# Raising the scheduling priority of PSUM evacuations, and a third buffer for gate and rotation, in a two-layer hybrid attention block

## The chip, the cores and the metric

The kernel runs on one core of one Trainium2 chip. The metric is the device time of one execution in microseconds (us), the median over several runs. The instructions are issued on five in-order engines: PE (matrix products and transposes, results in PSUM), ACT (pointwise functions and copies), DVE (vector arithmetic and reductions), POOL (elementwise arithmetic on SBUF) and SP (which only issues DMAs here).

## The reference, cut to what matters

Two layers act on 512 latent tokens and 256 context tokens of width 1024. Each layer normalises, projects once to 3584 columns, runs three groups of attention heads on parts of the projection, multiplies each group's output with a gate, and projects back:

```
h  = rms_norm(x, norm_g[l]) * (1 + sc) + sh          # same for the context: hc
qa, ka, va, ga, qb, kb, vb, gb, qn, kn, vn, gn = split_proj(h @ w_in[l])
ya = rms_norm(diff_attend(rope(qa), rope(ka), va)) * silu(ga)     # group A, 4 heads, two maps each
yb = gqa_attend(rope(qb), rope(kb), vb) * silu(gb)                # group B, 6 heads, 2 key heads
yn = neighbourhood_attend(qn, kn, vn, bias) * silu(gn)            # group C, 6 heads
x  = x + gt * (concat(ya, yb, yn) @ w_out[l])
```

q and k are normalised per head (rms_norm) first; queries of the latents also read the keys of the context. In the first layer the context gets its own attention and update; in the second only its keys and values are needed.

## The kernel before, in words

**Projection.** Tokens are cut into six tiles of 128 (j = 0 to 3 latent, 4 and 5 context), and the columns into ten chunks of 256 or 384 (`CH`, L37): a0 and a1 hold q, k, v of group A, b0 and b1 of B, c0, c1 and c2 of C, and ga, gb and gn the three gates. `proj` (L709) takes one chunk and one token tile at a time. It takes a PSUM tile with the tag "p" (`psP`, two buffers, L122), issues 24 products into it (`mm3`, L676: high and low parts of activations and weights, three products for each of eight slices of 128 input features), and calls `evac` (L657), which empties the tile. Weights arrive as pieces in a ring (`WStream`, L60): a DMA, a rounding copy on ACT (L89) and a subtraction on POOL or DVE (L92).

**Evacuation.** What reads the PSUM tile depends on the chunk:
- `qk_evac` (L451), for q and k: one ACT copy to the SBUF tile "xn" (L462). Then the square (L464) into "sq", its sum (L465), and the rotation in `qk_turn` (L477): two POOL products into a tile "tb" (L485, L487), one product (L489) and one sum that reads "tb" (L490). Every two tiles an inverse root (L163) is formed on POOL, and `qk_finish` (L494) scales, splits to 16 bits and issues a transposing DMA (L534).
- `v_evac` (L573), for v: an ACT scaling to 16 bits (L585) and a DVE operation that forms the rest (L586).
- `gate_evac` (L597), for the gates: tanh on ACT into a tile "sq" (L600), then a DVE operation that reads "sq" and the PSUM tile and writes a tile "tb" (L602); for ga one more product on POOL (L605); then a DMA stores "tb" to DRAM (L606). It is read back when the heads' output is gated (`gate_load`, L961).

The tag "tb" has two buffers. The rotation, the gates, the modulation blocks at the start (`ada_pair`, L196) and some residual loads (L1122) share them. The tags "xn" and "sq" have five and two.

**Heads.** `attn` (L972) goes through units of one head and 128 queries (the context's units hold several heads; a head of group A has two maps): scores on PE (`stage_S`, L780), their maximum on DVE (L827, or L824 with bias) and its scaling on ACT (L829), the exponential on ACT (L841), a rounding to 16 bits on ACT (L861) and the rest on POOL (L862), a transposing DMA (L864), the product with v on PE (`stage_PV`, L867), and the output arithmetic in `pv_evac` (L903). For group A a DVE operation (L857) first combines the two maps.

**Order.** `both` (L1064) writes the heads of one group and the projection of the next chunks alternately: during A the chunks b0, b1, gb; during B c0, c1, c2, gn; during C the output projection. That is only the order in which instructions are written down. Each one gets a number that grows along this order, and the order of each engine is fixed before the run by a simulated timeline: an engine that is free takes, of the instructions whose inputs and buffers are ready in that simulation, the one with the lowest number. A `prio(off)` around a call (L132) adds `off` to the numbers of the instructions issued inside. Before the change this is used for `stage_S` (-400), for `y_build` and `y_pair` (-600), for the next layer's `build_h` (-800) and for one prefetch (-100). The evacuations have their plain numbers. On the chip every engine works through its list in that order, and waits where an input is late.

Of the kernel before, what the change touches and what calls it, by code (L numbers as in the profile page):

```python
# [10 lines left out]
F32 = mybir.dt.float32  # L11
# [4 lines left out]
AF = mybir.ActivationFunctionType  # L16
ALU = mybir.AluOpType
# [99 lines left out]
def tile_hybrid_block(ctx: ExitStack, tc: tile.TileContext, xT_d, cT_d, ng_d, w_ada, bT_d, w_in, w_out,  # L117
# [7 lines left out]
    V, A, G, PE, SP = nc.vector, nc.scalar, nc.gpsimd, nc.tensor, nc.sync  # L125
# [3 lines left out]
    def sb(shape, dt=F32, tag="", bufs=1):  # L129
        return pool.tile(shape, dt, tag=tag, bufs=bufs, name=tag)  # L130

    def prio(off):  # L132
        def deco(f):
            def g(*a, **k):
                tc.cur_priority += off
                try:
                    return f(*a, **k)
                finally:
                    tc.cur_priority -= off
            return g  # L140
        return deco

    ident = sb([128, 128], F32, "ident")
    ones = sb([128, 128], F32, "ones")
    colD = sb([128, 1], F32, "colD")
# [33 lines left out]
    def new_mods(l):  # L179
        mods[l] = (sb([128, KT, 2], F32, "mA", 2), sb([128, KT, 2], F32, "mB", 2), sb([128, KT, 2], F32, "mG", 2))  # L180
# [15 lines left out]
    def ada_pair(load):  # L196
        l, bs, ts = load
        if l not in mods:
            new_mods(l)
        ps = psV.tile([128, 512], F32, tag="pv", name="ada")  # L200
        for i in range(2):
            for r in range(2):
                for g in range(4):
                    PE.matmul(ps[32 * g:32 * g + 32, 128 * i:128 * i + 128], lhsT=cS[:, 4 * r + g, :],
                              rhs=ts[2 * i + r][:, g, :], start=(r == 0), stop=(r == 1), tile_position=(0, 32 * g))
        t = sb([128, 256], F32, "tb", 2)
        V.tensor_copy(t, ps[:, 0:256])
        for i in range(2):
            PE.matmul(ps[:, 256 + 2 * i:258 + 2 * i], lhsT=t[:, 128 * i:128 * i + 128], rhs=sel, start=True, stop=True)
        for i, b in enumerate(bs):  # L210
            w, kt = divmod(b, 8)
            src = ps[:, 256 + 2 * i:258 + 2 * i]
            if w == 1:
                V.tensor_scalar(out=mods[l][0][:, kt, :], in0=src, scalar1=bT1[:, l, kt:kt + 1],
                                scalar2=ng[:, l, kt:kt + 1], op0=ALU.add, op1=ALU.mult)
            else:
                V.tensor_scalar(out=mods[l][1 if w == 0 else 2][:, kt, :], in0=src, scalar1=bT[:, l, b:b + 1],
                                scalar2=None, op0=ALU.add)
# [64 lines left out]
    for l in range(DEPTH):  # L283
        for c in ORDER:
            n, c0 = CH[c][1], sum(v[1] for k, v in CH.items() if k < c)
            pidx[l, c] = []
            for q in range(4):
                src = w_in[l, q, :, 2 * c0:2 * c0 + 2 * n].rearrange("p (k n) -> p k n", n=n)
                pidx[l, c].append(len(pieces))
                pieces.append(("w", n, 2, [(src, 0, n)]) + ((v_norm(l, c, q),) if c in VCOL else ()))  # L290
        for part in ("ab", "n"):
            for oc in range(4):
                pidx[l, part, oc] = []
                for k0, nk in OKT[part]:
                    src = w_out[l, oc, :, k0:k0 + nk, :]
# [150 lines left out]
    def bc(ap, shape):  # L446
        return ap.to_broadcast(shape)
# [3 lines left out]
    def qk_evac(l, g, w, j, ps, last, tag=None):  # L451

        d = 32 if g == "A" else 64
        nh = 2 if (g, w) == ("B", "k") else NH[g]
        n = nh * d
        b = batch.setdefault((g, w), [])
        if not b:
            b.append(sb([128, 24], F32, "ss", 4))
        ss = b[0]
        i = len(b) - 1  # L460
        xt = sb([128, 384], F32, "xn", 5) if tag is None else sb([128, 768], F32, *tag)[:, 0:384]
        A.copy(out=xt[:, :n], in_=ps)  # L462
        sq = sb([128, 384], F32, "sq", 2)
        A.activation(out=sq[:, :n], in_=xt[:, :n], func=AF.Square, scale=QS)  # L464
        V.tensor_reduce(out=ss[:, nh * i:nh * i + nh], in_=sq[:, :n].rearrange("p (h d) -> p h d", d=d),  # L465
                        axis=AX.X, op=ALU.add)
        b.append((j, xt))
        qk_turn(l, g, w, j, xt, nh, d)
        if not last:
            return  # L470
        del batch[g, w]
        m = (len(b) - 1) * nh
        r = rsqrt(ss[:, :m], m, 1.0, d * EPS * QS * QS)
        for i, (j, xt) in enumerate(b[1:]):
            qk_finish(l, g, w, j, xt, r[:, nh * i:nh * i + nh], nh, d)

    def qk_turn(l, g, w, j, xt, nh, d):  # L477

        c, n = lc[l], nh * d
        xn = xt[:, :n].rearrange("p (h d) -> p h d", d=d)  # L480
        if g in "AB" and j < 4:
            t1, t2 = c["T", g, w]
            h = d // 2
            tb = sb([128, 384], F32, "tb", 2)[:, :n].rearrange("p (h d) -> p h d", d=d)
            G.tensor_tensor(out=tb[:, :, 0:h], in0=xn[:, :, h:d], in1=bc(t2[:, j:j + 1, 0:h], [128, nh, h]),  # L485
                            op=ALU.mult)
            G.tensor_tensor(out=tb[:, :, h:d], in0=xn[:, :, 0:h], in1=bc(t2[:, j:j + 1, h:d], [128, nh, h]),  # L487
                            op=ALU.mult)
            share("T").tensor_tensor(out=xn, in0=xn, in1=bc(t1[:, j:j + 1, :], [128, nh, d]), op=ALU.mult)  # L489
            share("R").tensor_tensor(out=xn, in0=xn, in1=tb, op=ALU.add)  # L490
        elif (g, w) != ("C", "q"):
            G.tensor_tensor(out=xn, in0=xn, in1=bc(c["g"][g + w].unsqueeze(1), [128, nh, d]), op=ALU.mult)
# [80 lines left out]
    def v_evac(l, c, g, j, ps, h0, nh):  # L573
        s = st[g]
        if (l, c) not in scaled:
            scaled.add((l, c))
            a = v_scale(l, c)
            for h in range(h0, h0 + nh):
                s["si", h] = a[:, 6:7]
                s["si2"] = a[:, 5:6]  # L580
            s["s", c] = a[:, 7:8]
        sc = s["s", c]
        src = ps.rearrange("p (h d) -> p h d", d=64)
        hi, lo = s["V"][:, j, h0:h0 + nh, 1:65], s["V"][:, j, h0:h0 + nh, 65:129]
        A.activation(out=hi, in_=src, func=AF.Copy, scale=sc)  # L585
        V.scalar_tensor_tensor(out=lo, in0=src, scalar=sc, in1=hi, op0=ALU.mult, op1=ALU.subtract)  # L586

    gates = set()

# [7 lines left out]
    def gate_evac(l, c, j, ps):  # L597
        f0, n = GCOL[c]
        t = sb([128, 384], F32, "sq", 2)[:, :n]
        A.activation(out=t, in_=ps, func=AF.Tanh, scale=0.5)  # L600
        y = sb([128, 384], F32, "tb", 2)[:, :n]
        V.scalar_tensor_tensor(out=y, in0=t, scalar=1.0, in1=ps, op0=ALU.add, op1=ALU.mult)  # L602
        if c == "ga":
            y4 = y.rearrange("p (h d) -> p h d", d=64)
            G.tensor_tensor(out=y4, in0=y4, in1=bc(lc[l]["sub"].unsqueeze(1), [128, 4, 64]), op=ALU.mult)  # L605
        SP.dma_start(out=g_d[l][128 * j:128 * j + 128, f0:f0 + n], in_=y)  # L606
        gates.add((l, c, j))
# [495 lines left out]
    def out_parts(l):  # L1103

        if l + 1 == DEPTH:
            for h in range(2):
                st["part", h] = (big(1, F32, [128, KT // 2, NL]) if h else
                                 st["stB"][:, 0:2048].rearrange("p (k t) -> p k t", t=NL))
                for q in range(2):
                    SP.dma_start(out=st["part", h][:, 2 * q:2 * q + 2, :], in_=x1_d[:, 4 * h + 2 * q:4 * h + 2 * q + 2, :])  # L1110
        for oc in range(4):
            if oc == 1 and l + 1 < DEPTH:
                layer_consts(l + 1)
                h_bound(l + 1)
            for st_ in range(2 if l == 0 else 1):
                _, t0, w = streams[st_]
                for b in range(2):
                    db = 2 * oc + b
                    if l + 1 == DEPTH:
                        xo = st["part", db // 4][:, db % 4, :]  # L1120
                    else:
                        xo = sb([128, 576], F32, "stg", 2) if st_ == 0 else sb([128, 384], F32, "tb", 2)  # L1122
                        xo = xo[:, 0:w]
                        SP.dma_start(out=xo, in_=xT_d[:, db, t0:t0 + w])
                    ps = psP.tile([128, 512], F32, tag="p", name="op")
                    out_mm(ps, l, "ab", oc, b, st_, b == 1 and (st_ == 1 or l))
                    V.scalar_tensor_tensor(out=xo, in0=ps[:, 0:w], scalar=mods[l][2][:, db, st_:st_ + 1], in1=xo,
                                           op0=ALU.mult, op1=ALU.add)
                    if l + 1 < DEPTH:
                        SP.dma_start(out=part_d[:, db, t0:t0 + w], in_=xo)  # L1130
                    yield
                    yield
# [238 lines left out]
```

## Time and profile before

| what | value |
|---|---|
| median of 3 runs | 922.99 us (919.12 to 923.62) |
| the profiled execution | 921.41 us |
| its span, from first to last instruction | 919.6 us |
| mean granted TensorE clock | 0.957 of full speed |
| busy ACT, POOL | 593.1 us (64%), 544.1 us (59%) |
| ACT exponential L841, 200 instructions | 166.3 us |
| POOL rest of the probabilities L862, 138 instructions | 205.4 us |

The page gives the busy time of every engine as a share of the span. A view by windows gives the same for any stretch, with the granted clock of PE beside it. The view of waits lists which instruction waited for which, with the total, the number of times and the longest. The timeline shows single instructions with their start and duration; in brackets stands the idle time before one and what ended it. PEld are the weight loads of PE, which run beside its products.

### The profile page before, as it was taken

What the parts mean: (1) busy time and instruction counts of PE and PEld (TensorE: products, weight loads), DVE (VectorE), ACT (ScalarE), POOL (GpSimd) and SP (SyncE); (2) the same over time, 40 slices, a digit from 0 to 9 for tenths busy, and PEclk for the clock granted to TensorE, in tenths of its full rate; (3) what the DMA queues carried; (4) which work ended last, traced back from release to release, by engine and by line L of the source; (5) the groups of instructions that cost most, each with busy time, mean ns of one, the idle gap of its engine ahead of it and who ended that gap; (6) DMA issues with size and microseconds to landing.
All of it is one profiled execution on the core that took longest, in us unless ns stands there. A gap on an engine that the chain in (4) does not pass through costs nothing. (4 is left out here: it accounts for less than half of the span.)

```text
span 919.6 us, 17947 instructions
## 1 busy us (share of the span) xinstructions
PE 824.1 (90%) x6386; PEld 705.7 (77%) x6386; DVE 681.9 (74%) x1306; ACT 593.1 (64%) x1269; POOL 544.1 (59%) x503
## 2 busy tenths in 40 slices
PE   6898988896998899896999989989959999987988
PEld 3687877795987688784778879978848878875667
DVE  4985787988778866557755798789977976876743
ACT  5334577785887687577663445478758888878630
POOL 1638855899698565434421036939988886654310
PEclk9999998998999999998999989999979999998999
DMA  9924895645879997998798723784547789999642
GB/s 325 320 88 127 202 198 151 139 102 136 190 156 212 223 213 178 223 262 217 145 232 245 246 76 92 173 206 98 123 131 188 133 199 255 205 233 250 129 87 88
DMA packets 307193, 165.46 MB, mean 180 GB/s; under 512 B 256544, under 2 KB 275232, under 8 KB 306976
## 3 DMA queue, kind: packets, MB, share of 16 engines
q1 hardware_dynamic: 307104, 164.33, 74.5%
q8 instruction: 50, 0.82, 0.4%
q14 instruction: 39, 0.32, 0.1%
HBM read 86.55 MB, written 15.47 MB: 111 GB/s over the span
## 5 line engine op out<-in xcount | busy, mean ns | idle before, releaser
L862 POOL TENSOR_TENSOR hl<-p,hl 128x768 f16<-128x768 f32 (+3 forms) x138 | 205.4, 1492 | 170.7 <-ACT hl L861 159.0
L679 PE MATMUL proj<-whi,bigL 128*128 128x384 f32 (+1 forms) x592 | 203.0, 344 | 8.5 <-DVE tb L602 5.1
L680 PE MATMUL proj<-wlo,bigL 128*128 128x384 f32 (+1 forms) x592 | 199.6, 337 | 0.8 <-POOL wlo L92 0.7
L681 PE MATMUL proj<-whi,bigL 128*128 128x384 f32 (+1 forms) x592 | 196.7, 334 | 0.0
L841 ACT ACTIVATE p<-sc,nb,gsc 128x768 f32<-128x768 f32 (+3 forms) x200 | 166.3, 845 | 10.9 <-DVE p L857 4.6
L827 DVE TENSOR_REDUCE mx<-sc 128x1 f32<-128x768 f32 (+2 forms) x128 | 118.6, 931 | 30.3 <-PE sc L775 30.3
L861 ACT CAST hl<-p 128x768 f16<-128x768 f32 (+3 forms) x144 | 104.4, 725 | 46.4 <-DMA pt<-hl 29.9
L679 PEld LDWEIGHTS proj<-whi,bigL 128*128 128x128 f32 x592 | 115.0, 194 | 18.9 <-DVE tb L602 7.2
L680 PEld LDWEIGHTS proj<-wlo,bigL 128*128 128x128 f32 x592 | 115.6, 195 | 3.9 <-POOL wlo L92 1.5
L681 PEld LDWEIGHTS proj<-whi,bigL 128*128 128x128 f32 x592 | 114.5, 194 | 2.7 <-issue 1.6
L92 POOL TENSOR_TENSOR wlo<-raw,whi 128x768 fp32r<-128x768 f32 (+1 forms) x44 | 82.8, 1889 | 31.7 <-ACT whi L89 28.1
L89 ACT CAST whi<-raw 128x768 fp32r<-128x768 f32 (+1 forms) x104 | 80.1, 779 | 25.3 <-DMA raw<-in_w_in_dram 11.1
L897 PEld LDWEIGHTS <-pt 128*128 128x128 f16 x736 | 66.4, 100 | 36.8 <-DMA pt<-hl 23.2
L679 PE MATMUL proj<-whi,bigC 128*128 128x384 f32 (+2 forms) x224 | 75.6, 337 | 1.0 <-ACT xn L462 1.0
L92 DVE TENSOR_TENSOR wlo<-raw,whi 128x768 fp32r<-128x768 f32 (+1 forms) x60 | 61.5, 1028 | 19.4 <-ACT whi L89 18.1
L680 PE MATMUL proj<-wlo,bigC 128*128 128x384 f32 (+2 forms) x224 | 74.3, 332 | 0.0
L163 POOL TENSOR_TENSOR rsqb<-rsqb,half 128x12 f32<-128x12 f32 (+2 forms) x25 | 68.5, 2739 | 9.7 <-DVE rsqb L162 8.8
L681 PE MATMUL proj<-whi,bigC 128*128 128x384 f32 (+2 forms) x224 | 73.6, 331 | 0.0
L898 PEld LDWEIGHTS <-pt 128*128 128x128 f16 x736 | 66.8, 100 | 4.6 <-issue 2.4
L775 PE MATMUL sc<-bigL 128*128 128x512 f16 (+4 forms) x184 | 46.5, 314 | 18.5 <-ACT p L841 18.1
L897 PE MATMUL pv<-vA,pt 128*128 128x128 f16 (+2 forms) x424 | 52.1, 230 | 12.1 <-DMA pt<-hl 12.1
L829 ACT ACTIVATE nb<-mx,lnp,gsc 128x1 f32<-128x1 f32 (+1 forms) x104 | 39.9, 385 | 33.3 <-DVE mx L827 22.5
(327 smaller groups left out, 2038.6 us busy)
## 6 DMA issues: line engine op xcount, KB each, us to landing
raw<-in_w_in_dram SPq DMA_DIRECT2D x64, 384.0 KB, 3.9
adw<-in_w_ada_dram SPq DMA_DIRECT2D x68, 256.0 KB, 3.5
raw<-in_w_out_dram SPq DMA_DIRECT2D x16, 384.0 KB, 4.5
raw<-in_w_in_dram SPq DMA_DIRECT2D x16, 256.0 KB, 3.0
g_d<-tb SPq DMA_DIRECT2D x20, 192.0 KB, 2.8
gt<-g_d SPq DMA_DIRECT2D x18, 192.0 KB, 3.6
hl<-in_w_ada_dram SPq DMA_DIRECT2D x12, 256.0 KB, 4.8
pt<-in_w_ada_dram SPq DMA_DIRECT2D x12, 256.0 KB, 4.9
```

Of the source, the lines that this page charges most:

```text
L89: self.nc.scalar.copy(out=hi, in_=raw2)
L92: self.share("W").tensor_tensor(out=lo, in0=raw2, in1=hi.bitcast(F32), op=ALU.subtract)
L163: G.tensor_tensor(out=y, in0=x, in1=half[:, 0:n], op=ALU.pow)
L679: PE.matmul(ps, lhsT=xh, rhs=hi, start=(kt == 0), stop=False)
L680: PE.matmul(ps, lhsT=xh, rhs=lo, start=False, stop=False)
L681: PE.matmul(ps, lhsT=xl, rhs=hi, start=False, stop=(kt == KT - 1))
L827: V.tensor_reduce(out=mx[:, 0:ns], in_=ps[:, 0:w * ns].rearrange("p (a b) -> p a b", b=w), axis=AX.X, op=ALU.max)
L841: A.activation(out=p[:, w * x:w * x + w], in_=u["ps", i][:, w * x:w * x + w], func=AF.Exp, bias=u["nb", i][:, x:x + 1], scale=lc[l]["sc"][ ...
L861: A.copy(out=hl[:, 0:n], in_=p)
L862: lo_eng.tensor_tensor(out=hl[:, n:2 * n], in0=p, in1=hl[:, 0:n], op=ALU.subtract)
L897: PE.matmul(po[r, :], lhsT=pt[:, b, r], rhs=V_[:, vt, c0:129], start=first, stop=False)
L898: PE.matmul(po[r, 0:65 - c0], lhsT=pt[:, nb + b, r], rhs=V_[:, vt, c0:65], start=False, stop=stop)
```

## The change

Five instructions that read a projected tile in PSUM are issued through `first = prio(-1200)`: the copy of q and k, both operations of v, and tanh and the product of the gate. Their numbers drop by 1200, below those of all the heads' operations near them, `stage_S` with its -400 included. The square, the rotation and all that follows keep their numbers. The tag "tb" gets three buffers in place of two, wherever it is used.

```
+    first = prio(-1200)
@@ ada_pair @@
-        t = sb([128, 256], F32, "tb", 2)
+        t = sb([128, 256], F32, "tb", 3)
@@ qk_evac @@
-        A.copy(out=xt[:, :n], in_=ps)
+        first(A.copy)(out=xt[:, :n], in_=ps)
@@ qk_turn @@
-            tb = sb([128, 384], F32, "tb", 2)[:, :n].rearrange("p (h d) -> p h d", d=d)
+            tb = sb([128, 384], F32, "tb", 3)[:, :n].rearrange("p (h d) -> p h d", d=d)
@@ v_evac @@
-        A.activation(out=hi, in_=src, func=AF.Copy, scale=sc)
-        V.scalar_tensor_tensor(out=lo, in0=src, scalar=sc, in1=hi, op0=ALU.mult, op1=ALU.subtract)
+        first(A.activation)(out=hi, in_=src, func=AF.Copy, scale=sc)
+        first(V.scalar_tensor_tensor)(out=lo, in0=src, scalar=sc, in1=hi, op0=ALU.mult, op1=ALU.subtract)
@@ gate_evac @@
-        A.activation(out=t, in_=ps, func=AF.Tanh, scale=0.5)
-        y = sb([128, 384], F32, "tb", 2)[:, :n]
-        V.scalar_tensor_tensor(out=y, in0=t, scalar=1.0, in1=ps, op0=ALU.add, op1=ALU.mult)
+        first(A.activation)(out=t, in_=ps, func=AF.Tanh, scale=0.5)
+        y = sb([128, 384], F32, "tb", 3)[:, :n]
+        first(V.scalar_tensor_tensor)(out=y, in0=t, scalar=1.0, in1=ps, op0=ALU.add, op1=ALU.mult)
@@ out_parts @@
-                        xo = sb([128, 576], F32, "stg", 2) if st_ == 0 else sb([128, 384], F32, "tb", 2)
+                        xo = sb([128, 576], F32, "stg", 2) if st_ == 0 else sb([128, 384], F32, "tb", 3)
```

## The prediction

> **What bounds the kernel now.** I read the page's head first, then the busy time by windows, then who PE waits for, and last the timeline at the two places that stand out. The head:
>
> ```profile
> span 919.6 us, 17947 instructions
> PE 824.1 (90%) x6386; PEld 705.7 (77%) x6386; DVE 681.9 (74%) x1306; ACT 593.1 (64%) x1269; POOL 544.1 (59%) x503
> ```
>
> PE is busy 90% of the span and no other engine over 74%. Time is lost where PE stands still, 919.6 - 824.1 = 95.5 us in all. The windows say where. Columns: stretch, its length, busy us of PE, PEld, DVE, ACT and POOL with counts, granted PE clock, DMA share, GB/s.
>
> ```profile
> core 0: us, PE busy (x) PEld busy (x) DVE busy (x) ACT busy (x) POOL busy (x), PEclk, DMA share, GB/s
> 140.00:250.00 110.00, 95.47 (x696) 85.73 (x696) 94.46 (x143) 81.53 (x203) 89.76 (x90) 0.95 0.61 136
> 250.00:345.00 95.00, 89.17 (x733) 75.23 (x734) 73.14 (x144) 75.96 (x145) 70.84 (x60) 0.98 0.91 202
> 595.00:700.00 105.00, 87.13 (x656) 76.79 (x655) 91.33 (x137) 77.38 (x183) 83.62 (x86) 0.92 0.64 153
> 700.00:800.00 100.00, 96.85 (x758) 85.31 (x757) 75.19 (x109) 85.81 (x152) 76.69 (x57) 1.00 0.90 196
> 214.00:222.00 8.00, 2.81 (x12) 1.89 (x12) 6.25 (x7) 4.49 (x10) 8.00 (x5) 0.86 0.60 172
> 222.00:228.00 6.00, 5.92 (x22) 5.92 (x23) 4.90 (x6) 3.17 (x7) 5.76 (x5) 0.62 0.80 197
> 670.00:683.00 13.00, 3.10 (x19) 1.42 (x18) 8.55 (x10) 7.58 (x19) 13.00 (x11) 0.64 0.42 106
> 683.00:688.00 5.00, 5.00 (x17) 5.00 (x18) 4.94 (x7) 1.45 (x4) 4.04 (x4) 0.56 0.54 141
> ```
>
> The heads of group A run in the first and the third stretch, and PE stands 14.5 and 17.9 us there; the stretches behind them lose 5.8 and 3.2 us. Most of A's idle time lies in two holes: 214 to 222 (8.00 - 2.81 = 5.2 us) and 670 to 683 (13.00 - 3.10 = 9.9 us). After each hole PE is busy throughout, at a granted clock of 0.62 and 0.56. What PE waits for, over the whole span (total, times, longest):
>
> ```profile
> PE sc L775 <- ACT p L841: 20.2, 18, 3.9
> PE pv L897 <- DMA pt<-hl: 16.7, 21, 3.1
> ...
> PE proj L679 <- DVE tb L602: 5.1, 4, 2.8
> PE yt L640 <- DVE tb L602: 4.4, 1, 4.4
> ...
> PE proj L679 <- ACT xn L462: 2.1, 4, 1.0
> ```
>
> Evacuations are named for under 12 us, the heads' chain for 36.9. But a wait on the heads is a wait only because PE had nothing else in its list at that place. The second hole shows why it had nothing. PE first:
>
> ```profile
> 662.72 0.34 PE L681 MATMUL proj<-whi,bigL 128*128 128x384 f32 x1
> ...
> 663.24 0.34 PE L681 MATMUL proj<-whi,bigL 128*128 128x384 f32 x1
> ...
> 682.97 0.69 PE L679 MATMUL proj<-whi,bigL 128*128 128x384 f32 x1 [2.79 <-DVE tb L602]
> ```
>
> The first gate tile (gb, token tile 0) is complete at 663.24 + 0.34 = 663.6. One slice of three products takes 663.24 - 662.72 = 0.52 us, so a tile of eight slices takes 4.2. The next-but-one tile, which needs the same PSUM buffer, starts at 682.97, when L602 has emptied it. The evacuation of that first tile:
>
> ```profile
> 671.34 0.48 ACT L600 ACTIVATE sq<-proj 128x384 f32<-128x384 f32 x1
> ```
>
> ```profile
> 682.37 0.54 DVE L602 SCALAR_TENSOR_TENSOR tb<-sq,proj 128x384 f32<-128x384 f32 x1
> ```
>
> Tanh starts 671.34 - 663.58 = 7.8 us after the products, behind the heads' ACT work. Then 682.37 - 671.82 = 10.6 us pass before L602, although DVE is idle for 4.4 of the 13 us in this hole. What holds L602 is its output buffer:
>
> ```profile
> 651.85 0.65 POOL L485 TENSOR_TENSOR tb<-xn,t2Bq 128x192 f32<-128x192 f32 x1
> ...
> 657.78 0.91 POOL L485 TENSOR_TENSOR tb<-xn,t2Bq 128x192 f32<-128x192 f32 x1
> ...
> 666.02 0.99 POOL L490 TENSOR_TENSOR xn<-xn,tb 128x384 f32<-128x384 f32 x1
> ...
> 675.88 0.58 POOL L485 TENSOR_TENSOR tb<-xn,t2Bq 128x192 f32<-128x192 f32 x1
> ...
> 679.45 0.99 POOL L490 TENSOR_TENSOR xn<-xn,tb 128x384 f32<-128x384 f32 x1
> ```
>
> A rotation holds "tb" from L485 to its L490. Two are open from 657.78 on, so both buffers are taken; the one freed at 667.0 is kept for the rotation of 675.88, which was written down earlier than the gate, and the other is free at 680.4. L602 follows 2 us later. In the first hole the same two gate tiles are held; there tanh comes at 221.0 and L602 at 221.5 and 224.1:
>
> ```profile
> L600 ACT ACTIVATE sq<-proj x3: 478/480/491, 221.0 to 228.6; 128x384 f32<-128x384 f32 x3
> ```
>
> ```profile
> L602 DVE SCALAR_TENSOR_TENSOR tb<-sq,proj x2: 553/554/555, 221.5 to 224.1; 128x384 f32<-128x384 f32 x2
> ```
>
> **The change, part by part.** It adds no instruction and removes none; it moves five kinds of them forward in the lists of ACT and DVE and gives "tb" a third buffer.
>
> (1) The holes, 5.2 + 9.9 = 15.1 us. With the priority, tanh of the first gate tile follows the product at about 664; with the third buffer L602 follows tanh; the PSUM tile is free near 665 in place of 682.9, and PE, done with the second gate tile before the hole, has the third and fourth to fill it with: 2 x 4.2 = 8.4 us of the 9.9, and one tile covers most of the 5.2. What is late next is the weights of the following chunk, whose L92 is on POOL, and POOL is busy 13.00 of 13.00 us in this hole. Work done early counts in full only if PE is the bound where it comes from: it is busy 96.85 of 100 us from 700 to 800 and 89.17 of 95 from 250 to 345. I take two thirds, 10.1 us; the bounds are 0 and 15.1.
>
> (2) The clock behind the holes. 6 us at 0.62 and 5 us at 0.56 lose 6 x 0.38 + 5 x 0.44 = 4.5 us against a full clock. It goes with (1): 3.0 us, bounds 0 and 4.5. The Trainium skill (TensorE: Matmul & The Clock Gate, "Part 1: The HAM clock gate") says that the clock halves after an idle window of about 3.4 us and returns after a busy one; an estimate from that page is 2 x 1.7 = 3.4 us for two holes, two thirds of which would make the forecast 0.7 us later. The trace agrees in direction, 0.62 and 0.56 behind the holes against 1.00 from 700 to 800.
>
> (3) The two named waits outside the holes: L640, an output transpose that needs the PSUM buffer of the last gate tile (4.4), and the copies L462 (2.1), 6.5 us. An evacuation still has to wait for the instruction in progress and to run, so I take half, 3.3; bounds 0 and 6.5.
>
> (4) The price. Each evacuation now goes ahead of the heads' exponential, maximum and rounding. Durations (min, median, max in ns), and what ACT waited for in these instructions:
>
> ```profile
> L462 ACT COPY xn<-proj x56: 243/460/488, 81.5 to 800.2; 128x384 f32<-128x384 f32 x32, 128x256 f32<-128x256 f32 x12, 128x128 f32<-128x128 f32 x12
> L600 ACT ACTIVATE sq<-proj x30: 362/478/514, 113.1 to 830.4; 128x384 f32<-128x384 f32 x20, 128x256 f32<-128x256 f32 x10
> ...
>   PE proj L681: 17.4, 15
> ```
>
> One such step puts 0.46 to 0.48 us ahead of the exponential; take 0.47. PE waits 18 + 21 = 39 times for the heads' chain. If an evacuation lengthened each, 39 x 0.47 = 18.3 us; a gain is not excluded, since q and k of the next group are ready earlier, but no row gives it a size and I bound it at 0. A quarter of the waits is my choice, because ACT is idle 36% of the span and most exponentials have slack: 4.6 us lost.
>
> With one answer: the copies and v outside these places, and the stores L606, which move forward on SP with the gates, add nothing; PE's busy time covers them (96.85 of 100 us in the fourth stretch), and without that cover they would be in (3). The rotation keeps its number, so POOL's list changes little. The third buffer costs only memory.
>
> Sum: 10.1 + 3.0 + 3.3 - 4.6 = 11.8 us. The profiled execution took 921.41 us (span 919.6), 1.6 below the median of 922.99; so 909.6 for such an execution, and 911.2 for the median.
>
> **The rivals.**
>
> *POOL bounds the holes: no change.* For it: POOL is busy 13.00 of 13.00 and 8.00 of 8.00 us in the holes. The heads there cannot end sooner, and if PE's work brought forward only leaves a later gap, (1) and (2) vanish: 923.0 - 3.3 + 4.6 = 924.3. Against it: PE, not POOL (76.69 of 100), is fullest in the stretch behind. The Trainium skill (Perfetto Trace Analysis, "Identifying the Most-Contended Engine") says to optimise the engine of highest occupancy first; in these holes that is POOL, which this change leaves alone, so by that rule this rival wins. 0.18.
>
> *ACT stands before an evacuation: slower.* ACT's list is fixed from a simulated timeline. An evacuation taken early in the simulation, whose products come later on the chip, stops ACT with the heads' maxima scaling, exponentials and roundings queued behind it, and PE, DVE and POOL wait for those. The last row above says that this happens now: 15 times, 17.4 us, 1.16 each. If half of the 56 + 30 evacuations above came early, that is 43 - 15 = 28 more, 32.5 us of ACT, and at the quarter used in (4) 8.1 us of PE; with the holes left open because the order elsewhere shifts, 923.0 + 8.1 = 931.1. It decides from 16 more early evacuations on (16 x 1.16 / 4 = 4.6 us) if the holes stay; if they close, it would take 57 to eat the 16.4 us of (1) to (3). Against it: ACT is free 36% of the span. 0.15.
>
> *The priority does nothing, only the buffer works.* If at each moment no lower number stood ready, the lists stay as they are. Then tanh stays at 671.34, L602 follows at about 671.9, and PE can fill the hole from 672.4 on; in the first hole L602 is not held by a buffer and nothing changes. Of the 11 us from 672 on PE is idle at least 11 - 3.1 = 7.9; two thirds of that and of the clock loss of 2.2 are 6.8 us: 916.2. Against it: the 7.8 us before tanh. 0.10.
>
> **How the numbers follow.** My forecast has 0.57. Its best case takes all upper bounds, 15.1 + 4.5 + 6.5 = 26.1 us: 896.9. Its worst case without any gain and with the full price is 941.3, beyond the rivals. A range of 897 to 926 takes in the best case, the third rival and the first one with its neighbourhood; it leaves out the slower rival (0.15) and little else. About 0.5%, or 4.6 us, is what a measurement of this kernel can tell from no change, so faster means below 918.4 and slower above 927.6. Faster is most of the forecast (0.54) and most of the buffer rival (0.08): 0.62. Within 0.5% lies the first rival and what remains of the two: 0.23. Slower is the second rival: 0.15.
>
> **What would show it right or wrong.** Right: L602 of the first gb tile of either layer starts within 2 us of its products; no window near the holes with PE under half busy; the granted clock near 1.00 behind them; the wait of L640 on L602 under 2 us. Wrong: POOL full and PE idle at another place for as long; ACT's wait for "PE proj L681" well over 17.4 us, or PE's waits for L841 and for the transposed probabilities over 36.9 by more than the holes gave. A rotation that takes the third buffer ahead of the gate would show as L600 early and L602 late.

## The result and the profile after

The changed kernel takes 934.44 us (median of 5 runs, 929.1 to 939.7); the kernel before, run beside it, 921.31. The ratio is 1.0149, with an interval of [1.0123, 1.0174]: the change costs about 13.7 us, where 11.8 us of gain were forecast. (The ratios here and below come from all runs of a comparison; they are not the quotients of the two medians and differ from these by up to 0.24%.) The profiled execution is the fastest of the five, 929.1 us with a span of 927.3: it shows 7.7 us of the loss, and what the median loses beyond that is in no trace. In the kernels with the change, code lines are 3 higher than before (scores L778, products with v L900, exponential L844), and what is issued through `first` is recorded under L137, the call inside `prio`. The head of the page after:

```profile
span 927.3 us, 17924 instructions
...
PE 824.2 (89%) x6386; PEld 703.7 (76%) x6386; DVE 678.3 (73%) x1306; ACT 592.6 (64%) x1269; POOL 546.4 (59%) x503
```

Every engine is busy for about as long as before, PE to within 0.1 us and the others to within 4; PE's idle time grew from 95.5 to 103.1 us. The same windows as before, in the same columns:

```profile
core 0: us, PE busy (x) PEld busy (x) DVE busy (x) ACT busy (x) POOL busy (x), PEclk, DMA share, GB/s
140.00:250.00 110.00, 95.86 (x671) 85.75 (x671) 88.83 (x132) 80.42 (x193) 93.88 (x88) 0.94 0.57 130
250.00:345.00 95.00, 84.79 (x693) 71.93 (x690) 70.52 (x149) 70.28 (x146) 65.18 (x59) 0.96 0.91 196
595.00:700.00 105.00, 93.17 (x737) 82.32 (x736) 86.08 (x143) 76.75 (x183) 88.49 (x87) 0.98 0.69 159
700.00:800.00 100.00, 92.02 (x680) 80.52 (x678) 76.34 (x109) 82.18 (x148) 74.25 (x61) 0.95 0.82 186
...
214.00:222.00 8.00, 7.27 (x52) 6.68 (x51) 6.52 (x10) 4.53 (x11) 8.00 (x6) 1.00 0.90 209
222.00:228.00 6.00, 6.00 (x36) 5.72 (x35) 5.61 (x6) 2.62 (x8) 5.83 (x5) 1.00 0.49 104
...
670.00:683.00 13.00, 8.73 (x56) 7.14 (x56) 10.88 (x13) 9.67 (x23) 12.84 (x11) 1.00 0.50 137
683.00:688.00 5.00, 5.00 (x30) 5.00 (x31) 3.98 (x5) 2.29 (x6) 5.00 (x4) 1.00 0.30 77
```

Both holes are largely filled: PE is busy 7.27 of 8 us (before 2.81) and 8.73 of 13 (before 3.10), and the granted clock behind them is 1.00 in place of 0.62 and 0.56. The windows stand at fixed times while the work has moved, so I also count by events: the ends of the second and the third gb tile lie 6.0 us apart in layer 0 (before 12.0) and 7.7 in layer 1 (before 20.5). But the first stretch as a whole has only 0.4 busy us more than before (95.86 against 95.47), and the two stretches that were fullest lost more than the third one gained (93.17 in place of 87.13): 250 to 345 has 84.79 busy us in place of 89.17, 700 to 800 has 92.02 in place of 96.85. PE's waits after:

```profile
PE pv L900 <- DMA pt<-hl: 25.7, 25, 3.1
PE sc L778 <- ACT p L844: 10.6, 10, 2.1
PE yt L621 <- DVE o L945: 9.4, 4, 4.2
...
PE yt L643 <- DVE tb L137: 3.5, 2, 3.3
...
PE proj L682 <- DVE vA L137: 3.2, 1, 3.2
PE proj L682 <- ACT xn L137: 2.7, 5, 0.9
...
PE proj L682 <- DVE tb L137: 1.5, 1, 1.5
```

The waits on the heads' chain are 25.7 + 10.6 = 36.3 us (before 36.9), those on their output (L945) grew from 2.2 to 9.4. Of the waits on evacuations, the projection's on the gate fell from 5.1 to 1.5 and the output transpose's (L643) from 4.4 to 3.5; those on the copies (2.1 before, 2.7 now) and on v (0.9 before, 3.2 now) grew. Nothing here is 14 us long: waits do not tell where this loss is. Following the same instruction through both traces does. I count instructions of a kind in order and compare their starts; numbers are us, behind the first column as deviations from before.

| event | before | after |
|---|---|---|
| 1st exponential | 112.2 | +4.2 |
| 17th exponential | 165.4 | +10.1 |
| 73rd | 355.1 | +11.9 |
| 121st | 604.5 | +10.2 |
| 145th | 695.4 | +12.3 |
| 193rd | 861.0 | +7.4 |
| last product of projection tile 31 | 239.2 | -6.8 |
| last product of projection tile 79 (first gb tile of layer 1) | 663.6 | +9.2 |
| last product of projection tile 82 | 696.4 | -2.1 |
| last product of projection tile 102, the last one | 826.3 | +8.7 |
| span | 919.6 | +7.7 |

Right behind the two holes the projection is ahead of before, by 6.8 us at 239; elsewhere in the table it is late like the heads, which run late from their first exponential on. By 165 us, ahead of the first hole, they are 10.1 us late, more than the 7.7 that this execution loses in all; at the later places of the table it is 7 to 12.

What changed ahead of the first exponential is POOL's list. Before, and then after (start, duration, instruction):

```profile
86.94 0.75 POOL L490 TENSOR_TENSOR pt<-pt,tb 128x256 f32<-128x256 f32 x1
...
88.33 0.48 POOL L485 TENSOR_TENSOR tb<-xn,t2Aq 128x128 f32<-128x128 f32 x1
88.74 0.48 POOL L487 TENSOR_TENSOR tb<-xn,t2Aq 128x128 f32<-128x128 f32 x1
89.16 0.75 POOL L490 TENSOR_TENSOR hl<-hl,tb 128x256 f32<-128x256 f32 x1
92.39 2.91 POOL L163 TENSOR_TENSOR rsqb<-rsqb,half 128x16 f32<-128x16 f32 x1 [2.47 <-DVE rsqb L162]
```

```profile
87.64 0.46 POOL L488 TENSOR_TENSOR tb<-xn,t2Aq 128x128 f32<-128x128 f32 x1
88.05 0.46 POOL L490 TENSOR_TENSOR tb<-xn,t2Aq 128x128 f32<-128x128 f32 x1
88.47 0.46 POOL L488 TENSOR_TENSOR tb<-xn,t2Aq 128x128 f32<-128x128 f32 x1
88.89 0.47 POOL L490 TENSOR_TENSOR tb<-xn,t2Aq 128x128 f32<-128x128 f32 x1
89.31 3.35 POOL L166 TENSOR_TENSOR rsqb<-rsqb,half 128x16 f32<-128x16 f32 x1
92.63 0.77 POOL L493 TENSOR_TENSOR hl<-hl,tb 128x256 f32<-128x256 f32 x1
```

Before, POOL opens one rotation of q (t2Aq) and then closes k's last one (hl<-hl,tb, 89.16). After, the third buffer lets it open two of q, and an inverse root of 3.35 us goes in as well; k's last rotation closes at 92.63, 3.5 us later. What follows from it is late too. The first two lines are the issues of k's last transpose of a latent tile and of q's first, before; then the same after:

```profile
96.72 1.24 SPq L534 DMA_TRANSPOSE bigL<-stg  x1
...
104.47 1.24 SPq L534 DMA_TRANSPOSE bigL<-stg  x1
```

```profile
99.58 1.24 SPq L537 DMA_TRANSPOSE bigL<-stg  x1
...
107.67 1.24 SPq L537 DMA_TRANSPOSE bigL<-stg  x1
```

So k's last latent tile is sent 2.9 us later and q's first 3.2, and the first scores start at 111.8 in place of 108.2.

### The profile page after: what moved, and what is told of

Read it like the earlier page. It is cut to its first block, busy times and chain, and to the rows that moved or that the text cites. A ratio compares the mean times of both kernels' runs of the same rounds, so it can differ in the third digit from the quotient of the medians.

```text
span 927.3 us, 17924 instructions
## 1 busy us (share of the span) xinstructions
PE 824.2 (89%) x6386; PEld 703.7 (76%) x6386; DVE 678.3 (73%) x1306; ACT 592.6 (64%) x1269; POOL 546.4 (59%) x503
## 5 line engine op out<-in xcount | busy, mean ns | idle before, releaser
L844 ACT ACTIVATE p<-sc,nb,gsc 128x768 f32<-128x768 f32 (+3 forms) x200 | 166.4, 845 | 11.3 <-DVE p L860 4.7
L900 PEld LDWEIGHTS <-pt 128*128 128x128 f16 x736 | 68.2, 102 | 47.9 <-DMA pt<-hl 34.7
L92 POOL TENSOR_TENSOR wlo<-raw,whi 128x768 fp32r<-128x768 f32 (+1 forms) x44 | 84.4, 1925 | 13.3 <-ACT whi L89 11.4
L901 PEld LDWEIGHTS <-pt 128*128 128x128 f16 x736 | 68.1, 102 | 4.3 <-issue 1.7
L900 PE MATMUL pv<-vA,pt 128*128 128x128 f16 (+2 forms) x424 | 53.3, 232 | 16.9 <-DMA pt<-hl 16.6
L501 DVE TENSOR_TENSOR xn<-xn,rsqb 128x384 f32<-128x384 f32 (+1 forms) x44 | 51.8, 1200 | 8.2 <-POOL rsqb L166 7.3
```

The costliest lines, as they stand in the source:

```text
L92: self.share("W").tensor_tensor(out=lo, in0=raw2, in1=hi.bitcast(F32), op=ALU.subtract)
L844: A.activation(out=p[:, w * x:w * x + w], in_=u["ps", i][:, w * x:w * x + w], func=AF.Exp, bias=u["nb", i][:, x:x + 1], scale=lc[l]["sc"][ ...
L900: PE.matmul(po[r, :], lhsT=pt[:, b, r], rhs=V_[:, vt, c0:129], start=first, stop=False)
L901: PE.matmul(po[r, 0:65 - c0], lhsT=pt[:, nb + b, r], rhs=V_[:, vt, c0:65], start=False, stop=stop)
```

## The experiments

Three theories were on trial. **Theory 1**: the third buffer is the loss, because rotations take it and change POOL's list, first at the start. **Theory 2**: the priority is the loss, by putting evacuations ahead of the heads. **Theory 3**: any new order costs by chance. Times are medians, ratios are to before in the same comparison, with intervals of 95%.

**The parts.** `first = prio(0)` with "tb" at 3:

> The third buffer of tb alone, all evacuations at their plain numbers. Theory 1 (the third buffer lets POOL open rotations of q before it closes those of k, the heads start late, and the heads' chain sets the end): the first exponential starts near 116 us as after the change, not near 112, and the time is 925 to 934 us. Theory 2 (the priority sets evacuations ahead of the heads' work and slows their chain everywhere): as before, 918 to 924 us, first exponential near 112.

`first = prio(-1200)` with "tb" back at 2:

> The priority of -1200 alone, tb with two buffers. Theory 1: the first exponential starts near 112 us and the time is 915 to 923 us. Theory 2: 930 to 938 us, with the heads' exponentials falling behind step by step through both layers. Theory 3 (neither part by itself, the lists are reshuffled and only the pair is slow): both this and the buffer alone within 0.5% of before.

The gates write to a tag of their own, `y = sb([128, 384], F32, "tg", 1)`, the rest has "tb" at 2:

> The priority, and a buffer of their own for the gates (a new tag with one buffer); the rotations, the modulation and the residual loads keep two buffers of tb, so POOL's rotations cannot take the third. Theory 1: the heads start as before (near 112 us), the gates no longer wait for rotations, 908 to 921 us. Theory 2: 930 to 938 us as with the change.

"tb" at 3, `first(l)` with -1200 in layer 1 and 0 in layer 0:

> The third buffer throughout, the priority in the second layer only. Theory 1: the delay comes in the first layer with the buffer, so 925 to 934 us, within 4 us of the buffer alone, since the heads' chain and not PE sets the end in the second layer. If PE sets the end there (the reasoning of the prediction), the hole near 670 us closes and it is 8 us or more faster than the buffer alone. Theory 2: half of the loss, 925 to 929 us, and slower than the buffer alone.

Buffer alone 942.88, ratio 1.0217 [1.0172, 1.0262]; priority alone 926.52, 1.0057 [1.0024, 1.0090]; one gate tile of its own 934.44, 1.0127 [1.0066, 1.0188]; the third buffer with the priority in layer 1 only 944.93, 1.0245 [1.0182, 1.0308]. The buffer alone loses more than the pair; the priority costs 0.6% by itself and takes some of the buffer's loss back, and it seems to do that in layer 0, since in layer 1 alone it takes nothing back (layer 0 alone was not run). With the buffer alone the first exponential is 5.9 us late, with the priority alone 0.4 early. With one gate tile the start is intact, but that tile is held until its store is done, and the fifth ga tile ends 11 us late. Theory 1 had the sign at the start right in all four, but not the sizes: it had 925 to 934 us for the buffer alone and 908 to 921 for the gate tile.

**Offsets and other buffers.** An offset of 50 in place of 1200, with "tb" at 2 and at 3:

> Priority alone (tb 2) with an offset of 50 in place of 1200: a tile's own few instructions ahead of its neighbours, not ahead of the heads' work of a group that was emitted long before. Theory 2 (the priority slows the heads' chain): most of the loss of the priority alone goes, 920 to 924. Theory 3 (only the order that happens to come out matters): anywhere between 915 and 940, and the first exponential off before's 112.2 by less than 1 us. Theory 1 has no loss to explain here beyond the rotation and says 920 to 927.

> The change with an offset of 50 in place of 1200, tb at 3. With tb at 2 the offset of 50 cost nothing and the one of 1200 0.6%. If the loss of the change is the third buffer's and the priority takes some of it back at any size: 930 to 938, first exponential about 4 us late as in the change. If it takes the large offset to take it back: 938 to 946. If the loss were the large priority's: 921 to 926.

The gate's product written over its tanh (`y = t`), "sq" at 3, "tb" at 2, with offsets of 1200, 50 and 0:

> Priority as in the change, but the third buffer goes where rotations cannot take it: tb keeps 2, the gate's product is written over its tanh in sq, and sq gets 3. Theory 1 (the third tb buffer lets POOL open q rotations ahead of k's closing steps, and the single gate buffer of the kernel with a gate tile of its own blocked PSUM): the first exponential starts within 1 us of before's 112.2, the first gb tile of each layer gets its L602 within 2 us of its products, and the time is that of the priority alone or better, 915 to 926. Theory 2 (the priority slows the heads' chain everywhere): as the priority alone or slower, 926 to 935, the exponentials drifting late through layer 0. Theory 3 (any new order of the lists costs some 5 to 15 us at the c1 chunk of layer 1): 930 to 940, the start intact and the tiles of c1 late.

> Gates written in place (sq 3, tb 2) with an offset of 50 in place of 1200. If the large offset is what cost 1.1% in that pair: within 0.5% of before, 917 to 926, the start intact. If it is the gates leaving sooner, so that PE runs ahead and DVE's list takes the next group's rounding before the heads' maxima: 926 to 935, with PE's wait for the exponentials over 3 us somewhere from 720 to 760.

> The kernel before with the gates written in place alone (sq 3, tb 2, no priority): a buffer more for the gates that rotations cannot take. If the loss of the third buffer alone (2.2%) is all in the rotations that take it: within 0.5% of before, 917 to 926, with the second PE hole (before: 670 to 683) shorter, because the gate's product no longer waits for a rotation's buffer. If gates that leave PSUM sooner cost by themselves: 926 to 940.

Ratios to before, by buffer and offset:

| | 0 | 50 | 1200 |
|---|---|---|---|
| "tb" 2 | 1 | 1.0007 [0.9987, 1.0027] | 1.0057 [1.0024, 1.0090] |
| "tb" 3 | 1.0217 [1.0172, 1.0262] | 1.0240 [1.0206, 1.0275] | 1.0149 [1.0123, 1.0174] |
| "sq" 3, gate in place | 1.0123 [1.0088, 1.0158] | 1.0106 [1.0067, 1.0145] | 1.0114 [1.0068, 1.0160] |

The row decides, not the column. That speaks against theory 2, and against theory 3 in its plain form: neighbours in the table agree to 0.3% save for the offset of 1200. The offset of 50 does nothing measurable. My expectation for the gates in place (915 to 926 us) missed: their start is intact, yet they cost 1.1%; the three kernels take 931.50, 933.22 and 933.79 us. That lies where the rival expectations had it: gates that leave PSUM sooner let PE run ahead, and DVE's list then takes the next group's work before the heads' maxima. The sign named for it came as well, a wait of PE for the exponentials over 3 us between 720 and 760 (6.3 us with the offset of 50). Whether it is the cause is taken up below.

**The scale of v ahead as well.** `a = first(v_scale)(l, c)`, with the priority alone and with the gates in place:

> Priority alone (tb 2) plus the same priority on the chain that scales a chunk's v (L541 to L551), which the prioritised copies of v wait for. Theory: after layer 1's A heads, which end 7.6 us early with the priority alone, 10 us are lost because the first c1 tile waits from 738 to 746 for that chain; with it ahead, most of that stays: 917 to 922, exponential number 160 at or ahead of before's 755.9. Rival (the loss there is the wait for group A's heads to give vA free, not the chain): the first c1 tile still is copied at 746, 925 to 928.

> Priority, gates written in place with sq 3 and tb 2, and the v scale chain ahead as well. If the two theories (third buffer out of the rotations' reach; v scale chain) hold, their gains add: 908 to 920, faster than before. If any new order costs 5 to 15 us at c1: 925 to 940.

945.06, 1.0251 [1.0224, 1.0277], and 937.45, 1.0153 [1.0112, 1.0195]. That theory fell: with the chain ahead, group A's heads of layer 1 are 14 to 23 us late in the first of the two.

**The start put back.** The first try held k's last rotation and two of q's in the ada blocks' tile "adt":

> The changed kernel, with one thing held back at the start: in layer 0 the rotations of k's last tile and of two of q's take turns in a tile of their own (adt, one buffer, made as wide as they need), so that POOL has one q rotation, not two, and no rsqb of q ahead of k's last closing step; everything later has the third tb buffer and the priority. Theory 1 (this order at the start is where the change's loss begins): the first exponential starts within 1 us of before's 112.2 in place of 116.3, the sixteenth within 4 us of 165.4, and the time is 920 to 929. Theory 2 (the start costs little by itself, and the loss comes again at later places where PE runs ahead and the lists of DVE and POOL take its work first): 929 to 938 with the start intact, the exponentials drifting late later on, as with the gates written in place.

948.62, 1.0298 [1.0262, 1.0334]. POOL's order was as meant, but the ada blocks hold that tile, and POOL stood for it:

```profile
115.30 0.46 POOL L488 TENSOR_TENSOR adt<-xn,t2Aq 128x128 f32<-128x128 f32 x1 [11.55 <-PE ada L251]
```

It says nothing on the buffer, but one thing on the start: the first exponential is 18.3 us late, 14.1 more than with the change, and the ratio is 1.0298 - 1.0149 = 1.49%, 13.7 us, above the change's. A delay there runs through to the end.

The next four give the third buffer to some users only. A tile "tc" takes every third turn of those that may have it:

```
    def tb3(n, third):
        turn[0] += third
        return sb([128, n], F32, "tb", 2) if not third or turn[0] % 3 else sb([128, 384], F32, "tc", 1)[:, 0:n]
```

In the first two `third` is false in `ada_pair` and for group A's rotations of layer 0, and true elsewhere (offset 1200, then 0); in the third it is `l == 1`; in the fourth it is true for the gates alone, so that each third gate tile takes "tc":

> The changed kernel, but the third tb buffer (now a tile tc of its own, every third turn) is given out only after group A's rotations of layer 0; until then there are two, and POOL's list at the start is before's. Theory 1 (the change's loss is the start, carried to the end): first exponential within 1 us of before's 112.2, the sixteenth within 3 us of 165.4, time 920 to 928. Theory 2 (the third buffer costs at every place where rotations take it): 928 to 940 in spite of the start, with the loss showing later, near 295 or 747.

> The same without the priority. The third buffer alone lost 12 us to the sixteenth exponential and 9 more at 662 to 695. Theory 1: 930 to 936, the second part only. Theory 2: 938 to 948, as the third buffer alone.

> The changed kernel with the third tb buffer given out in layer 1 only, the priority everywhere. Theory 1 (in the change layer 1 loses nothing: its heads start 8 us late and end 7.7 late): as the priority alone or up to 8 us better by layer 1's hole, 916 to 928, the exponentials of layer 0 as with the priority alone. Theory 2: 930 to 942, with layer 1's heads losing 5 us or more after 604.

> The changed kernel with the third buffer for the gates alone (each third gate tile takes tc), rotations keep the two, priority everywhere. If only rotations that take the third buffer cost: 916 to 928. If gates that leave PSUM sooner cost by themselves, as with the gates written in place (931.5): 928 to 936, PE ahead at 696 by 8 us or more and behind again by 747.

- Two buffers at the start: 926.77, 1.0072 [1.0049, 1.0096], where the change has 1.0149. POOL's order at the start is before's, the first exponential +0.2 us, the 17th -2.3.
- The same without the priority: 934.55, 1.0141 [1.0124, 1.0158], where the buffer alone has 1.0217.
- Third buffer in layer 1 only: 926.73, 1.0053 [1.0027, 1.0079], as the priority alone.
- Third buffer for the gates only: 924.05, 1.0025 [1.0005, 1.0045].

The start is worth 1.0149 - 1.0072 = 0.77% with the priority and 1.0217 - 1.0141 = 0.76% without, 7 us both times. Theory 1 is right on it. Where the rotations and residual loads after the start may take it too, it costs 1.0072 - 1.0025 = 0.47% more than for the gates alone.

**What the closed holes are worth.** The third buffer for the gates only, with offsets of 50 and 0:

> The third buffer for the gates alone, with an offset of 50 in place of 1200. If the effects add (offset 1200 alone +0.57%, with the gates' buffer +0.25%, so the buffer gives -0.3%; offset 50 alone nothing): 917 to 921, faster than before by about 0.3%. If a hole that closes is worth nothing (group A's heads set the pace, on POOL, through it): 921 to 925, PE ahead at 696 and behind or level again by 747.

> The third buffer for the gates alone and no priority. If the gates' buffer alone does what of the change is worth doing: 917 to 921. If the closed hole is worth nothing: 921 to 925. If gates that leave PSUM sooner cost by themselves, as the gates written in place did without a priority (1.2%): 927 to 935.

919.80, 0.9964 [0.9937, 0.9991], and 920.22, 0.9970 [0.9946, 0.9995], 12 runs each. These are the fastest kernels of the study, 0.3% ahead of before; that is under the 0.5% of the prediction, and twelve runs are what brings both intervals below 1. They close a part of the second hole only: the ends of its two gate tiles lie 12.1 us apart (before 20.5), and in layer 0 11.7 and 11.8 (before 12.0). In the first, at the second hole and behind it (these kernels' lines are 7 higher than before's):

```profile
670.00:683.00 13.00, 8.76 (x43) 8.20 (x44) 6.74 (x8) 5.64 (x12) 12.78 (x11) 0.74 0.53 132
683.00:688.00 5.00, 5.00 (x40) 4.49 (x38) 5.00 (x9) 4.93 (x11) 3.29 (x3) 1.00 0.59 121
700.00:800.00 100.00, 90.40 (x708) 78.72 (x707) 75.29 (x110) 80.85 (x144) 70.85 (x55) 0.95 0.83 178
728.00:745.00 17.00, 9.66 (x60) 6.09 (x59) 13.12 (x19) 12.12 (x19) 12.23 (x8) 0.71 0.87 195
```

and the last of these windows before:

```profile
728.00:745.00 17.00, 14.80 (x112) 12.69 (x111) 10.87 (x23) 15.09 (x25) 14.62 (x13) 1.00 0.89 198
```

The hole holds 8.76 busy us in place of 3.10, a gain of 5.7. From 728 to 745 PE has 9.66 in place of 14.80 and a clock of 0.71 in place of 1.00, a loss of 5.1. This is how the traces show it; no run took the cause away to test it. The chunk behind c0, c1, is v of group C, and goes into the buffer "vA" that group A's heads still read. Before, PE's last product with that v, and ACT's first copy of c1:

```profile
732.34 0.19 PE L898 MATMUL pv<-vA,pt 128*128 128x64 f16 x1
```

```profile
737.50 0.59 ACT L585 ACTIVATE vA<-proj,vnc 128x384 f16<-128x384 f32 x1
```

With the gates' buffer and the offset of 50, PE, ACT and DVE there:

```profile
738.17 1.44 PE L782 MATMUL sc<-stB 128*128 128x512 f16 x4 [5.69 <-ACT p L848]
...
743.59 0.26 PE L905 MATMUL pv<-vA,pt 128*128 128x64 f16 x1
```

```profile
743.88 1.06 ACT L137 ACTIVATE vA<-proj,vnc 128x384 f16<-128x384 f32 x2 [0.32 <-PE pv L905]
```

```profile
731.74 4.06 DVE L505 TENSOR_TENSOR xn<-xn,rsqb 128x384 f32<-128x384 f32 x2 [0.87 <-POOL rsqb L170]
735.73 0.94 DVE L834 TENSOR_REDUCE mx<-sc 128x1 f32<-128x768 f32 x1
```

PE came 8 us early through c0, so c0's finishing (L505, two instructions, 4.06 us) stands on DVE ahead of a maximum of the heads (L834). The exponential waits for that maximum, and PE stands 5.69 us for the exponential, with A's last product behind it in its list. That product ends 11.3 us later than before, and the copy of c1, which needs "vA" free, waits for PE (0.32 us). The lead of 8 us at the end of c0 is a lag of 5.9 at the third tile of c1. The same instructions in eight kernels, as ends in us (the lag of the gate's product is its start, counted from the end of its tile's products):

| kernel | lag of the first gb product, layer 1 | c0 done | A's last product | third c1 tile done |
|---|---|---|---|---|
| before | 18.8 | 727.4 | 732.5 | 747.2 |
| offset 50, "tb" 2 | 18.8 | 730.5 | 735.7 | 750.1 |
| offset 1200, "tb" 2 | 16.2 | 730.8 | 732.1 | 756.0 |
| gates' buffer, offset 50 | 10.0 | 719.5 | 743.8 | 753.1 |
| gates' buffer, offset 0 | 10.1 | 722.5 | 746.8 | 755.9 |
| gates in place, offset 1200 | 6.7 | 717.1 | 742.8 | 752.2 |
| gates in place, offset 0 | 6.5 | 722.3 | 748.2 | 758.4 |
| the change | 9.5 | 729.9 | 750.3 | 759.1 |

In four kernels c0 is done 5 to 10 us before its time, and in all four A's last product comes 10 to 16 us late. The table fits a lead of the projection that is lost there, but it does not rank the kernels: with the gates' buffer and with the gates in place, both at offset 0, A and c1 end within 2.5 us of each other, and the ratios are 0.9970 and 1.0123. Nor is a late A the only way to a late c1: with the priority alone A ends on time (732.1), and ACT stands 3.25 us for the DMA of a weight piece ahead of c1's first copy.

## Why the prediction was wrong, point by point

**The failed step** is the last sentences of the part with one answer: "The rotation keeps its number, so POOL's list changes little. The third buffer costs only memory." I had named that the engines' lists are made from a simulated timeline in which an engine takes what is ready; a free buffer makes another rotation ready, whatever its number. The prediction looked for a rotation that takes the third buffer only at the gate ("L600 early and L602 late"); after the change the product follows its tanh there (681.41 and 682.23), and a good part of the harm is at the start, where no gate waits. The third buffer alone costs 2.17%, 20 us. Of this 0.76% is the start; the rest, 1.41%, comes behind it (net of what the gates gain), and with the priority it shrinks to 0.15% (1.0072 against 1.0057, which these runs do not tell from nothing). The way from before to the change, kernel by kernel, in percent: priority +0.57, third buffer for the gates -0.32, for the later rotations and residual loads +0.47, for the start +0.77, which ends at 1.49. The second step's two intervals overlap; those of the last two do not. From the forecast of -11.8 us to the 13.7 measured are 25.5 us, and by these steps some 11.4 of them are the buffer's price, which the sum put at nothing, some 10.2 the gain of (1) and (2) that did not come, and the rest (3) and (4).

**(1) and (2), the holes and the clock, 13.1 us.** The filling came. The product starts 0.5 us behind its tile in layer 0 (before 4.9) and 9.5 in layer 1 (before 18.8), so "within 2 us" was right in layer 0 only. In layer 1 tanh still starts 8.7 us behind the products, behind exponentials, roundings and a weight copy in ACT's list; why they stand there in spite of the priority was not taken apart. What the filling is worth is far less than 13.1 us. No run fills both holes and does nothing else. The gates' buffer fills a part of the second and gives 3.3 and 2.8 us (0.36% and 0.30%, with 50 and 0); of the first of the two the trace does not show where they lie, since its projection is behind before at c1's third tile (by 5.9 us) and still at its last tile (by 1.0). With the third buffer in layer 1 only, the second hole is nearly closed (8.8 us between the two tiles, 18.7 with the priority alone), and the time is the same (1.0053 against 1.0057), though there the rotations of layer 1 may take the buffer too. For that hole and the clock behind it the prediction had two thirds of 9.9 + 2.2, 8.1 us. What failed is those two thirds, with their condition that "PE is the bound where it comes from". PE was busiest from 700 to 800, but its lead could not pass c1, which waits for A's heads; with the gates' buffer and the offset of 50 the clock came back behind the hole and was lost again at 728 to 745. The prediction also read its windows too strongly: the two holes hold 15.1 of the 32.4 us that PE stands in A's stretches, which is not most of them.

**(3), the waits elsewhere, 3.3 us.** Not gained: L643 waits 3.5 us (before 4.4), the copies' wait is 2.7 (before 2.1).

**(4), the price, 4.6 us.** About right where it can be seen: 0.57% [0.24, 0.90] is 5.3 us for the priority alone, and with the gates' buffer 1200 against 50 differs by 0.61%. With three buffers for everyone its sign turns (1.0217 to 1.0149), and by the run with the priority in layer 1 only that is layer 0's doing; which instruction does it was not found.

**The rivals.** *POOL bounds the holes* had the better picture of them: POOL is busy 12.78 of 13 us also where PE has 8.76 busy us, and PE's work brought forward left a later gap. It did not see the start. The Trainium skill (Perfetto Trace Analysis, "Optimization Strategy") reads gaps that repeat on the engine that should be full as a possible shortage of buffers. The gap here comes once in each layer, and the runs agree for the gate that waited, 0.3% to be had; where rotations took the buffer too, 2.2% were lost, so here the measurement limits that reading. *ACT stands before an evacuation* had the right side and 931.1 us, but not the cause. Its sign, after:

```profile
  PE proj L684: 24.0, 21
```

That is 6.6 us and 6 times more than before's 17.4 and 15, not the 28 times more of its sum nor the 16 from which it decides, and the priority alone loses 0.57%. *Only the buffer works* was wrong in sign: the buffer alone is slower than the change.

What stays open: which users behind the start cost 1.41% without the priority, why the gates in place cost 1.1 to 1.2% where a tile that only gates can take gains 0.3% (squares can take the third "sq" as rotations can the third "tb", which fits but was not tried alone; PE's long wait for an exponential near 738 does not tell them apart, since the fastest kernel has it too, 5.69 us), and the further 6 us between the first exponential and the 17th, which go when the start is put back. For these parts chance in the order (theory 3) is not excluded.

## What to carry to other kernels

A buffer added to a tag is given to every user of the tag; where the order of engines is made from readiness, count what each user would start earlier, and what would then stand behind it in an in-order list, above all at the start, where a delay runs through to the end. Give the buffer to the one user whose wait you mean to remove, and time that alone. Before counting a filled gap as a gain, follow the lead to the first point where the engine must wait for the other chain (here a v buffer that is still read): a lead that ends there was worth 0.3% at most here, however busy the engine is in between.

## What the runs showed of the hardware

The inverse root on POOL is long for its size: 4.19 us for 128x24 and 2.91 us for 128x16, some 0.18 us per column, where a product of 128x256 takes 0.75. The one ahead of k's close after the change (89.31, 3.35 us) takes as long as four such products.
